# Conditioning steps in twos, filled waits between projection and MLP, last blocks computed half by half, in a float32 decoder step

## The chip, the cores and the metric

The kernel runs on one core of a Trainium2 chip. Its time is the device time of one execution in microseconds; the number to beat is the median of three executions. One of them is also recorded by the hardware profiler, and the times of single instructions below come from that recorded one.

## The reference

One inference step of a decoder layer in float32, width 2048, for 320 tokens at once: 256 of a prompt and 8 sequences of 8 new tokens. Two token mixers run side by side, HGRN2 (a recurrence with 8 heads of 128) and attention over a latent cache (MLA); their outputs are merged by sigmoid gates, projected, normalised and added to x. A squared-ReLU MLP of width 8192 follows, normalised and added in the same way. Shift, scale and gate of both halves come from a conditioning vector for each of the 9 sequences.

```python
mod = jax.nn.silu(c) @ w_ada[l] + b_ada[l]             # 2048 -> 12288, 9 rows
sh1, sc1, gt1, sh2, sc2, gt2 = split(mod, 6)
h = rms_norm(x, g_pre_mix) * (1 + sc1) + sh1
proj = h @ w_in                                        # HGRN2 and MLA inputs, gates
y_a = hgrn2(...) @ w_a_out
y_b = mla(...) @ w_b_out
merged = sigmoid(gate_a) * y_a + sigmoid(gate_b) * y_b
x = x + gt1 * rms_norm(merged @ w_o, g_post_mix)
h2 = rms_norm(x, g_pre_mlp) * (1 + sc2) + sh2
u = relu(h2 @ w_up)
x = x + gt2 * rms_norm((u * u) @ w_down, g_post_mlp)
```

## The kernel before

Everything large is a product of weights with activations that lie transposed on chip, 128 features by 320 tokens to a tile. `gemm` makes 256 output columns: for each 8 tiles of the inner dimension one load of 1 MB (`raw`, issued by SyncE, three buffers in `wraw`), split by ScalarE (`whi`, L151) and VectorE (`wlo`, L148) into a high and a low part in two pieces, each of four inner tiles, and then three matmuls for each tile and each of the two halves `m` of the columns (`mm3`). The two halves go in turn within an inner tile, so both are complete only with the last matmuls of a call.

The conditioning product `c @ w_ada` (`ada_gen`) is cut into 96 steps. In its later part a step is one load of 1 MB from the same three buffers and four matmuls of 32x512, which fill the four column groups of the array; the trace shows two rows for each of them, so a step is 8 rows named `aux<-raw,cT`. Every fourth step ends with a copy by ScalarE (`adarow`, L329), four transposes and a reduction on VectorE (L313). The steps are called from `tick`, after each 8 inner tiles of a `gemm` while `hook["every"]` is 1 (the HGRN stage: four head pairs `hp`, then two gate products), after each second while it is 2 (merge), and ten in a row between the output projection and the MLP, from a pool `fraw` of three buffers of their own. `tick` also advances the HGRN recurrence of the pair before by two pieces, so that its small matmuls (`X`, `qt,kt`, `rp`, `osq`) lie between those of the projections. The order of instructions on each engine is that in which a scheduler places them; `tc.issue_after(i)` holds an instruction behind `i`.

Between projection and MLP (the gap): `out_squares` squares the last output blocks and adds them to `ssum`, `out_tile` scales (`zg`) and transposes them, `out_store` copies them to `zt`, `tok_rstd` sums `ssum` over features by a matmul with ones and makes the reciprocal root `trr` (Ln on ScalarE at L220, Exp at L221, four small VectorE steps). The residual (`x`, L1337) is updated in six pieces, squared, turned into a second root `r`, scaled (L1348, back into `zt`), transposed and split to `gh`, `gl`, on which `w_up` starts. The last MLP chunk ends in the same chain, with `za` for the sum over chunks and `zu` for the output.

Of the kernel before, what the change touches and what calls it, by code (L numbers as in the profile page):

```python
# [1 line left out]

# [10 lines left out]
ALU = mybir.AluOpType  # L13
# [4 lines left out]
D = 2048  # L18
# [3 lines left out]
NS = NB * NT  # L22
N = NP + NS
P = 128
# [57 lines left out]
def tile_hgrn2_mla_step(  # L82
# [48 lines left out]
    def behind():  # L131

        return tc.issue_after(pe_last[0].ins)

    def mm(out, lhsT, rhs, start, stop):
# [8 lines left out]
    def add(out, a, b, eng=None):  # L144
        (eng or nc.vector).tensor_tensor(out=out, in0=a, in1=b, op=ALU.add)  # L145
# [52 lines left out]
    def gemm(w2d, kt0, nkt, c0, xh, xl, fine=False):  # L198

        ps = [bank(acc), bank(acc)]  # L200
        for r0 in range(0, nkt, 8):
            raw, rv = load_w(w2d, kt0 + r0, 8, c0, 256)
            for s in range(2):
                hv, lv = split_w(rv, 4 * s, 4, 256)
                for k in range(4):
                    kk = r0 + 4 * s + k
                    for m in range(2):
                        ms = slice(m * P, (m + 1) * P)
                        mm3(ps[m][:, 0:N], hv[:, k, ms], lv[:, k, ms], xh[:, kk], xl[:, kk],
                            kk == 0, kk == nkt - 1)  # L210
                if fine and s == 0:
                    advance(side["per"])
            tick()
        return ps
# [86 lines left out]
    araw = [sraw]  # L301

    turned = []

    def ada_turn():

# [10 lines left out]
    def ada_gen():  # L317

        for b0, nb in [(SC1, 2), (SH1, 2), (SC1 + 2, 2), (SH1 + 2, 2)] + \
                [(m + f, 4) for f in (4, 8, 12) for m in (SC1, SH1)] + [(b0, 4) for b0 in range(GT1, 96, 4)]:  # L320
            ps = bank()
            nk = 16 // nb
            for r0 in range(0, KF, nk):
                raw, rv = load_w(w_ada, r0, nk, b0 * P, nb * P, araw[0])
                for k in range(nk):
                    mm(ps[32 * (k % 4):32 * (k % 4 + 1), 0:nb * P], cT[:, r0 + k], rv[:, k], r0 + k < 4, r0 + k >= KF - 4)
# [901 lines left out]
    with pool("gt") as gt:  # L1228
        ah = gt.tile([P, NH, N], F32R, name="ah")
        al = gt.tile([P, NH, N], F32R, name="al")  # L1230
        bh = gt.tile([P, NH, N], F32R, name="bh")
        bl = gt.tile([P, NH, N], F32R, name="bl")
        for src, dh, dl in ((oB, bh, bl), (oA, ah, al)):
            for f0 in range(0, NH, 2):
                fs = slice(f0, f0 + 2)
                raw = dl[:, fs].bitcast(F32)
                nc.gpsimd.dma_start(out=raw, in_=src[:, fs])
                split(dh[:, fs], dl[:, fs], raw)
        hook["every"] = 2
        gates(4)  # L1240
        order = (2, 3, 4, 0, 1, 5, 6, 7)
        for n, g in enumerate(order):
            for w, vh, vl, nm in ((w_b_out, bh, bl, "gb"), (w_a_out, ah, al, "ga")):
                ps = gemm(w, 0, 8, 256 * g, vh, vl)
                s = gate[(nm, g)]
                for m in range(2):
                    mul(s[:, m], s[:, m], ps[m][:, 0:N])
            s, s2 = gate.pop(("gb", g)), gate.pop(("ga", g))
            add(s, s, s2, nc.gpsimd)
            split(mh[:, 2 * g:2 * g + 2], ml[:, 2 * g:2 * g + 2], s)  # L1250
            if n + 3 < 8:
                gates(order[n + 3])
# [20 lines left out]
    def out_tile(pl2, ps, f, m, m0, banks):  # L1273

        zg = pl2.tile([P, N], F32, name="zg")
        nc.scalar.activation(out=zg[:, 0:NP], in_=ps[:, 0:NP], func=AF.Copy, scale=mod[:, m0 + f, 0:1])
        mul(zg[:, NP:N].rearrange("p (b t) -> p b t", t=NT), ps[:, NP:N].rearrange("p (b t) -> p b t", t=NT),
            bc(mod[:, m0 + f, 1:9, None], [P, NB, NT]))
        for i, t0, n in TOK:
            dst = banks[0][:, m, i] if i < 2 else banks[1][0:NS, m]  # L1280
            transpose(dst, zg[:, t0:t0 + n], P)

    def out_banks():
        return bank().rearrange("p (m i c) -> p m i c", m=2, i=2), \
# [10 lines left out]
    def tok_rstd(pl, ssum):  # L1295
        ps = bank()
        for i, t0, n in TOK:
            mm(ps[0:n, i:i + 1], ssum[:, t0:t0 + n], ones[:, 0:1], True, True)
# [4 lines left out]
        mean_eps(xx[:, 0:2], ps[:, 0:2], D)  # L1303
        mean_eps(xx[0:NS, 2:3], ps[0:NS, 2:3], D)
        rstd_of(xx, tm, r)
        return r

    with pool("zp") as zp, pool("zp2", 2) as zp2, pool("fraw", 3) as fraw:
        zt = [zp.tile([P, D], F32, name=f"zt{i}") for i in range(3)]
# [2 lines left out]
        nc.sync.dma_start(out=x1[1], in_=x_prompt[0, P:NP])  # L1312
        nc.sync.dma_start(out=x1[2][0:NS], in_=xsm)
        for g in range(8):
            ps = gemm(w_o, 0, KF, 256 * g, mh, ml)
            bk = out_banks()
            for m in range(2):
                out_squares(zp2, ps[m][:, 0:N], 2 * g + m, ssum)
            for m in range(2):
                out_tile(zp2, ps[m][:, 0:N], 2 * g + m, m, GT1, bk)  # L1320
            lz = out_store(bk, zt, g)
            if g == 0:
                log_exp_tables(lz)
        r = tok_rstd(zp, ssum)
        araw[0] = fraw
        for _ in range(10):
            next(ada_steps)
        araw[0] = wraw
        ssq2 = zp.tile([P, 3, 2], F32, name="ssq2")
        xx2 = zp.tile([P, 3], F32, name="xx2")  # L1330
# [45 lines left out]
    with pool("ml1") as ml1, pool("ml2", 2) as ml2:  # L1376
# [4 lines left out]
        for c in range(NCH):  # L1381
            last = c == NCH - 1
            uh = ml2.tile([P, 8, N], F32R, name="uh")
            ul = ml2.tile([P, 8, N], F32R, name="ul")
            for g in range(4):
                ps = gemm(w_up, 0, KF, c * 1024 + 256 * g, gh, gl)
                for m in range(2):
                    u = ml2.tile([P, N], F32, name="u")
                    nc.scalar.activation(out=u, in_=ps[m][:, 0:N], func=AF.Relu)  # L1389
                    nc.scalar.activation(out=u, in_=u, func=AF.Square)  # L1390
                    split(uh[:, 2 * g + m], ul[:, 2 * g + m], u)
            if c == 5:
                hook["every"] = 0
                ada_turn()
                mod_gain(GT2, V_GPD, False)
            if last:
                gstack.close()
                tstack = ExitStack()
                tp = tstack.enter_context(pool("tp", 1, "right"))
                zt = [tp.tile([P, D], F32, name=f"zu{i}") for i in range(3)]  # L1400
            for g in range(8):
                ps = gemm(w_down, 8 * c, 8, 256 * g, uh, ul)
                bk = out_banks() if last else None
                for m in range(2):
                    f = 2 * g + m
                    if c == 0:
                        nc.scalar.copy(out=za[:, f], in_=ps[m][:, 0:N])
                    else:
                        add(za[:, f], za[:, f], ps[m][:, 0:N])
                    if last:  # L1410
                        out_squares(ml2, za[:, f], f, ssum)
                if last:
                    for m in range(2):
                        out_tile(ml2, za[:, 2 * g + m], 2 * g + m, m, GT2, bk)
                    out_store(bk, zt, g)
        r = tok_rstd(ml1, ssum)
        for q in range(4):
            fs = slice(q * 512, (q + 1) * 512)
            for i, t0, n in TOK:
# [37 lines left out]
```

## Time and profile before

| | us |
|---|---|
| median of three executions | 2150.62 (2146.13 to 2152.61) |
| profiled execution | 2150.7 |
| its span | 2148.8 |
| TensorE busy | 2097.8 (98%) |
| VectorE, ScalarE, GpSimd busy | 1075.0, 862.9, 167.6 |

The execution has 1.9 us around the span. The stages in the span: HGRN about 508 to 820, gates and merge to 1061, output projection to 1180, the gap to about 1231 where the first block of `w_up` ends, MLP to 2132, and a tail to the end. PE is the matmul stream of TensorE. A row of a timeline is a run of alike instructions: start, length of the run, engine, line, operation, output and inputs, count, and in brackets how long the engine stood idle before and what ended it. In the list of waits a row is who waited, for whom, the sum, the times and the longest. In the table of windows each row is a stretch with the busy time of each engine, the granted TensorE clock as a share of 2.4 GHz, and the load of the DMA engines.

### The profile page before, as it was taken

What the parts mean: (1) busy time and instruction counts of PE and PEld (TensorE: products, weight loads), DVE (VectorE), ACT (ScalarE), POOL (GpSimd) and SP (SyncE); (2) the same over time, 40 slices, a digit from 0 to 9 for tenths busy, and PEclk for the clock granted to TensorE, in tenths of its full rate; (3) what the DMA queues carried; (4) which work ended last, traced back from release to release, by engine and by line L of the source; (5) the groups of instructions that cost most, each with busy time, mean ns of one, the idle gap of its engine ahead of it and who ended that gap; (6) DMA issues with size and microseconds to landing.
All of it is one profiled execution on the core that took longest, in us unless ns stands there. A gap on an engine that the chain in (4) does not pass through costs nothing.

```text
span 2148.8 us, 34659 instructions
## 1 busy us (share of the span) xinstructions
PE 2097.8 (98%) x14605; PEld 1897.9 (88%) x14605; DVE 1075.0 (50%) x1673; ACT 862.9 (40%) x1312; POOL 167.6 (8%) x167
## 2 busy tenths in 40 slices
PE   6999999999999999999999899999999999999997
PEld 4788988557788889999999599999999999999996
DVE  3555854446665546533544633444444444444455
ACT  4332443334545434333344543424343433333343
POOL 0000101203332211000010000000000000000001
PEclk9999999999999999999999899999999999999998
DMA  9886554544776768766854555544544545445442
GB/s 291 310 291 228 175 192 140 214 132 138 240 233 209 244 215 273 240 196 221 274 162 144 189 177 178 155 145 149 157 141 154 153 143 155 147 148 157 144 151 70
DMA packets 327572, 401.69 MB, mean 187 GB/s; under 512 B 10984, under 2 KB 265528, under 8 KB 324600
## 3 DMA queue, kind: packets, MB, share of 16 engines
q1 hardware_dynamic: 301576, 362.82, 52.5%
q0 software_dynamic: 3584, 21.50, 2.9%
q10 hardware_dynamic: 22256, 15.16, 2.3%
q8 instruction: 115, 1.88, 0.4%
q14 instruction: 41, 0.34, 0.0%
HBM read 387.44 MB, written 12.01 MB: 186 GB/s over the span
## 4 chain that ended last, share of the span: by engine, by line
PE 87%; issue 4%; DVE 3%; DMA 3%; ACT 2%; POOL 1%; SPq 1%; DVEq 0%; ACTq 0%; POOLq 0%
PE acc L136 76%; PE aux L136 7%; PE aux L139 4%; DVE wlo L148 1%; ACT whi L151 1%; DMA raw<-in_w_in_dram 1%; DMA raw<-in_w_ada_dram 1%; POOL X L142 1%; DMA raw<-in_w_q_up_dram 1%; SPq L161 0%; DMA craw<-in_cache_ckv_dram,pidx 0%; DVE zu L1420 0%; DVE X L148 0%; DMA raw<-in_w_kv_up_dram 0%; DVE zg L142 0%
## 5 line engine op out<-in xcount | busy, mean ns | idle before, releaser
L148 DVE TENSOR_TENSOR wlo<-raw,whi 128x1024 fp32r<-128x1024 f32 (+1 forms) x493 | 604.0, 1230 | 704.2 <-ACT whi L151 703.6
L151 ACT CAST whi<-raw 128x1024 fp32r<-128x1024 f32 (+1 forms) x493 | 502.9, 1025 | 812.6 <-PE acc L136 681.7
L136 PE MATMUL acc<-hh,whi 128*128 128x320 f32 x1168 | 369.5, 317 | 2.5 <-DVE partb L145 1.2
L136 PE MATMUL acc<-hl,whi 128*128 128x320 f32 x1168 | 362.2, 310 | 0.0
L136 PE MATMUL acc<-hh,wlo 128*128 128x320 f32 x1168 | 361.9, 311 | 0.0
L136 PE MATMUL acc<-uh,whi 128*128 128x320 f32 x1024 | 316.7, 309 | 0.0
L136 PE MATMUL acc<-gh,whi 128*128 128x320 f32 x1024 | 316.7, 309 | 0.0
L136 PE MATMUL acc<-gh,wlo 128*128 128x320 f32 x1024 | 316.6, 309 | 0.0
L136 PE MATMUL acc<-gl,whi 128*128 128x320 f32 x1024 | 316.4, 309 | 0.0
L136 PE MATMUL acc<-uh,wlo 128*128 128x320 f32 x1024 | 316.1, 309 | 0.0
L136 PE MATMUL acc<-ul,whi 128*128 128x320 f32 x1024 | 316.1, 309 | 0.0
L136 PEld LDWEIGHTS acc<-hh,whi 128*128 128x128 f32 x1168 | 219.5, 188 | 33.7 <-issue 16.1
L136 PEld LDWEIGHTS acc<-hl,whi 128*128 128x128 f32 x1168 | 219.9, 188 | 2.4 <-DVE hl L148 0.8
L136 PEld LDWEIGHTS acc<-hh,wlo 128*128 128x128 f32 x1168 | 219.3, 188 | 3.0 <-DVE wlo L148 1.7
L136 PEld LDWEIGHTS acc<-gh,whi 128*128 128x128 f32 x1024 | 192.5, 188 | 1.9 <-ACT u L1390 0.8
L136 PEld LDWEIGHTS acc<-uh,whi 128*128 128x128 f32 x1024 | 192.6, 188 | 1.7 <-ACT u L1389 0.8
L136 PEld LDWEIGHTS acc<-gh,wlo 128*128 128x128 f32 x1024 | 192.6, 188 | 0.2
L136 PEld LDWEIGHTS acc<-gl,whi 128*128 128x128 f32 x1024 | 192.7, 188 | 0.0
L136 PEld LDWEIGHTS acc<-ul,whi 128*128 128x128 f32 x1024 | 192.4, 188 | 0.0
L136 PEld LDWEIGHTS acc<-uh,wlo 128*128 128x128 f32 x1024 | 192.4, 188 | 0.0
L136 PE MATMUL aux<-raw,cT 128*32 128x512 f32 (+1 forms) x832 | 117.0, 608 | 16.7 <-DVE tt L142 11.7
L145 POOL TENSOR_TENSOR ssum<-ssum,sqt 128x320 f32<-128x320 f32 x26 | 25.9, 997 | 981.3 <-ACT sqt L1270 980.3
(425 smaller groups left out, 2546.6 us busy)
## 6 DMA issues: line engine op xcount, KB each, us to landing
raw<-in_w_ada_dram SPq DMA_DIRECT2D x96, 1024.0 KB, 5.3
raw<-in_w_up_dram SPq DMA_DIRECT2D x64, 1024.0 KB, 5.7
raw<-in_w_down_dram SPq DMA_DIRECT2D x64, 1024.0 KB, 5.3
raw<-in_w_in_dram SPq DMA_DIRECT2D x60, 1024.0 KB, 5.3
raw<-in_w_o_dram SPq DMA_DIRECT2D x16, 1024.0 KB, 6.3
raw<-in_w_in_dram SPq DMA_DIRECT2D x20, 512.0 KB, 6.8
raw<-in_w_b_out_dram SPq DMA_DIRECT2D x8, 1024.0 KB
raw<-in_w_a_out_dram SPq DMA_DIRECT2D x8, 1024.0 KB, 5.3
```

What stands on the lines that cost most here:

```text
L136: pe_last[0] = nc.tensor.matmul(out, lhsT=lhsT, rhs=rhs, start=start, stop=stop)
L139: pe_last[0] = nc.tensor.transpose(out=out, in_=in_, identity=ident[:k, :k])
L142: (eng or nc.vector).tensor_tensor(out=out, in0=a, in1=b, op=ALU.mult)
L145: (eng or nc.vector).tensor_tensor(out=out, in0=a, in1=b, op=ALU.add)
L148: return (eng or nc.vector).tensor_tensor(out=out, in0=a, in1=b, op=ALU.subtract)
L151: nc.scalar.copy(out=hi, in_=src)
```

## The change

Three edits.

1. In the HGRN stage the conditioning steps are called two after every second tick, not one after every tick.
2. Between projection and MLP, two matmuls of 128x512 whose result nobody reads are put behind each of the steps 3 to 6 of the ten, and the copy `adarow` is held behind the Exp of the root. The steps of the gap are held behind the matmuls of the root (`pin`).
3. `gemm` gets `apart`: in the last 8 inner tiles of the last call, both pieces are split first, and then all matmuls of half 0 come before those of half 1. It is used for the last block of the projection and of the last MLP chunk. The last block's squares are no longer added to `ssum`; `tok_rstd` takes both tiles, and VectorE adds the second sum to the first. In the last chunk `out_tile` follows `out_squares` for each half.

```diff
-    hook = {"every": 0, "n": 0}
+    hook = {"every": 0, "n": 0, "do": 1}
...
-                next(ada_steps, None)
+                for _ in range(hook["do"]):
+                    next(ada_steps, None)
...
+            if apart and r0 == nkt - 8:
+                sp = [split_w(rv, 4 * s, 4, 256) for s in range(2)]
+                for m in range(2):
+                    ms = slice(m * P, (m + 1) * P)
+                    for k in range(8):
+                        hv, lv = sp[k // 4]
+                        mm3(ps[m][:, 0:N], hv[:, k % 4, ms], lv[:, k % 4, ms], xh[:, r0 + k], xl[:, r0 + k],
+                            r0 + k == 0, k == 7)
+                tick()
+                continue
...
-                    nc.scalar.copy(out=row[:, 0:nb * P], in_=ps[:, 0:nb * P])
+                    with behind_of(pinned[0]):
+                        nc.scalar.copy(out=row[:, 0:nb * P], in_=ps[:, 0:nb * P])
...
-    hook["every"] = 1
+    hook.update(every=2, do=2)
...
-        hook["every"] = 2
+        hook["do"] = 1
...
+            if f == KF - 1:
+                return t
...
+        for j, sq in enumerate(blocks):
+            for i, t0, n in TOK:
+                mm(ps[0:n, 3 * j + i:3 * j + i + 1], sq[:, t0:t0 + n], ones[:, 0:1], True, True)
+            for n, c0, c1 in ((P, 0, 2), (NS, 2, 3)):
+                if j == 0:
+                    mean_eps(xx[0:n, c0:c1], ps[0:n, c0:c1], D)
+                else:
+                    nc.vector.scalar_tensor_tensor(out=xx[0:n, c0:c1], in0=ps[0:n, 3 + c0:3 + c1], scalar=1.0 / D,
+                                                   in1=xx[0:n, c0:c1], op0=ALU.mult, op1=ALU.add)
...
-        for _ in range(10):
+        pinned[0], after_mm[0] = last_exp[0], pin
+        idle = bank(acc)
+        for n in range(10):
             next(ada_steps)
+            if 3 <= n < 7:
+
+                for _ in range(2):
+                    with behind():
+                        mm(idle, ident, cst[:, 0:512], True, True)
+                after_mm[0] = pe_last[0]
...
-                ps = gemm(w_down, 8 * c, 8, 256 * g, uh, ul)
+                ps = gemm(w_down, 8 * c, 8, 256 * g, uh, ul, apart=last and g == 7)
```

What SyncE issues at the end of the HGRN stage, before: weights of the projection (`in_w_in`) and of the conditioning (`in_w_ada`) alternate, one load each.

```order
L161 DMA raw<-in_w_ada_dram 128x4x512
L161 DMA raw<-in_w_in_dram 128x8x256
L161 DMA raw<-in_w_ada_dram 128x4x512
L161 DMA raw<-in_w_in_dram 128x8x256 x2
L161 DMA raw<-in_w_ada_dram 128x4x512
```

Now the loads come in twos, up to the last two of the stage.

```order
L165 DMA raw<-in_w_ada_dram 128x4x512 x2
L165 DMA raw<-in_w_in_dram 128x8x256 x2
L165 DMA raw<-in_w_ada_dram 128x4x512
L165 DMA raw<-in_w_in_dram 128x8x256 x2
L165 DMA raw<-in_w_ada_dram 128x4x512
```

The pairs take two of the three buffers one after the other.

TensorE in the first head pair of the recurrence, before. A count after x is of instructions; `X` and `qt,kt` are the recurrence, `acc` the projection.

```order
L136 MATMUL acc<-hh,wlo 128x320
L136 MATMUL aux<-raw,cT 32x512 x3
L136 MATMUL aux<-X 64x64 x10
L136 MATMUL aux<-qt,kt 64x64 x4
L136 MATMUL acc<-hh,whi 128x320
L136 MATMUL acc<-hl,whi 128x320
```

The same place now.

```order
L140 MATMUL acc<-hh,wlo 128x320
L140 MATMUL aux<-raw,cT 32x512 x7
L140 MATMUL aux<-X 64x64 x10
L140 MATMUL aux<-qt,kt 64x64 x4
L140 MATMUL acc<-hh,whi 128x320
L140 MATMUL acc<-hl,whi 128x320
```

The rest of a step stood before the recurrence's matmuls; now the rest of a step and a whole further one stand there.

TensorE in the gap, before, from the last matmul of the projection: `zg` transposes, `ssum` the sum for the root, `zt` the first transposes for the MLP.

```order
L136 MATMUL acc<-mh,wlo 128x320
L136 MATMUL aux<-raw,cT 32x512
L139 MATMUL aux<-ident,zg 128x128 x2
L139 MATMUL aux<-ident,zg 64x128
L139 MATMUL aux<-ident,zg 128x128 x2
L139 MATMUL aux<-ident,zg 64x128
L136 MATMUL aux<-cst,ssum 128x1 x2
L136 MATMUL aux<-cst,ssum 64x1
L136 MATMUL aux<-raw,cT 32x512 x7
L139 MATMUL aux<-ident,adarow 128x128 x4
L136 MATMUL aux<-raw,cT 32x512 x16
L139 MATMUL aux<-ident,adarow 128x128 x4
```

Now, from the last matmul of the projection to the end of steps 0 and 1, whose eight matmuls (1, 4 and 3) are in the piece.

```order
L140 MATMUL acc<-mh,wlo 128x320
L143 MATMUL aux<-ident,zg 128x128 x2
L143 MATMUL aux<-ident,zg 64x128
L140 MATMUL aux<-cst,ssum 128x1 x2
L140 MATMUL aux<-cst,ssum 64x1
L140 MATMUL aux<-cst,sqt 128x1 x2
L140 MATMUL aux<-cst,sqt 64x1
L140 MATMUL aux<-raw,cT 32x512
L143 MATMUL aux<-ident,zg 128x128 x2
L140 MATMUL aux<-raw,cT 32x512 x4
L143 MATMUL aux<-ident,zg 64x128
L140 MATMUL aux<-raw,cT 32x512 x3
```

And on from there, to the first transposes for the MLP.

```order
L143 MATMUL aux<-ident,adarow 128x128 x4
L140 MATMUL aux<-raw,cT 32x512 x8
L140 MATMUL acc<-cst,ident 128x512 x2
L140 MATMUL aux<-raw,cT 32x512 x4
L140 MATMUL acc<-cst,ident 128x512 x2
L140 MATMUL aux<-raw,cT 32x512 x4
L140 MATMUL acc<-cst,ident 128x512 x2
L143 MATMUL aux<-ident,adarow 128x128 x4
L140 MATMUL aux<-raw,cT 32x512 x4
L140 MATMUL acc<-cst,ident 128x512 x2
L143 MATMUL aux<-ident,zt_10108 128x128
```

The sum for the root stands ahead of step 0 now, with a second one (`sqt`) behind it. Steps 2 and 3 follow in one run (`x8`), two matmuls of 128x512 (`acc<-cst,ident`) stand behind each of the steps 3 to 6, and the transposes for the MLP follow the last two.

## Rows read from the trace of the kernel before

**Rows 1.** Waits of TensorE over the whole span.
```profile
PE aux L136 <- DMA raw<-in_w_ada_dram: 5.0, 4, 2.1
PE aux L139 <- DVE rp L1018: 3.1, 3, 1.8
PE aux L136 <- POOL X L142: 2.8, 2, 1.5
```

**Rows 2.** Timeline of TensorE around one conditioning step of the merge stage.
```profile
829.18 0.31 PE L136 MATMUL acc<-hl,whi 128*128 128x320 f32 x1
829.32 0.31 PE L136 MATMUL acc<-hh,wlo 128*128 128x320 f32 x1
829.56 1.07 PE L136 MATMUL aux<-raw,cT 128*32 128x512 f32 x8
830.56 0.41 PE L136 MATMUL acc<-hh,whi 128*128 128x320 f32 x1
```

**Rows 3.** Timeline of TensorE, a first piece of a step in the first head pair.
```profile
524.55 1.05 PE L136 MATMUL aux<-raw,cT 128*32 128x512 f32 x2
525.53 0.80 PE L136 MATMUL aux<-X 128*64 128x64 f32 x20
```

**Rows 4.** The tile `raw` on TensorE from 505 to 820: durations in ns, count.
```profile
L136 PE MATMUL aux<-raw,cT x224: 592/605/617, 514.7 to 814.8; 128*32 128x512 f32 x112
```

**Rows 5.** Timeline of TensorE in the gap.
```profile
1182.65 1.92 PE L136 MATMUL aux<-raw,cT 128*32 128x512 f32 x14
...
1189.04 1.06 PE L136 MATMUL aux<-raw,cT 128*32 128x512 f32 x8 [2.13 <-DMA raw<-in_w_ada_dram]
1191.74 1.71 PE L136 MATMUL aux<-raw,cT 128*32 128x512 f32 x8 [1.64 <-DMA raw<-in_w_ada_dram]
...
1200.02 5.04 PE L139 MATMUL aux<-ident,zt 128*128 128x128 f32 x16
```

**Rows 6.** Timelines of SyncE and ScalarE in the second head pair.
```profile
593.14 0.37 SPq L161 DMA_DIRECT2D raw<-in_w_in_dram  x1
598.57 2.00 ACT L151 CAST whi<-raw 128x1024 fp32r<-128x1024 f32 x2 [8.05 <-DMA raw<-in_w_in_dram]
```

**Rows 7.** All loads of `raw` from 505 to 820, from issue to landing.
```profile
DMA to landing us min/median/max: 5.1/5.3/5.6
```

**Rows 8.** Page, part 5: the low split on VectorE, count, busy time and mean.
```profile
L148 DVE TENSOR_TENSOR wlo<-raw,whi 128x1024 fp32r<-128x1024 f32 (+1 forms) x493 | 604.0, 1230 | 704.2 <-ACT whi L151 703.6
```

**Rows 9.** Timelines of ScalarE, VectorE and SyncE in the gap.
```profile
1184.62 0.59 ACT L329 COPY adarow<-aux 128x512 f32<-128x512 f32 x1 [1.10 <-PE aux L136]
...
1186.60 7.26 DVE L1337 SCALAR_TENSOR_TENSOR x<-zt,trr,x 128x1024 f32<-128x1024 f32 x6
...
1183.76 13.07 SPq L161 DMA_DIRECT2D raw<-in_w_ada_dram  x6
```

**Rows 10.** Windows of the gap.
```profile
1190.00:1192.00 2.00, 0.36 (x8) 0.16 (x8) 2.00 (x3) 1.91 (x5) 0.00 (x0) 1.00 1.04 386
1192.00:1194.00 2.00, 1.45 (x8) 0.00 (x0) 1.85 (x2) 1.92 (x5) 0.00 (x0) 0.51 1.05 389
1212.00:1214.00 2.00, 2.00 (x13) 0.61 (x13) 1.67 (x5) 1.64 (x3) 0.45 (x1) 0.87 0.00 0
```

**Rows 11.** Timeline of TensorE in the attention stage and behind the gap.
```profile
490.35 1.98 PE L136 MATMUL aux<-Ss,ckvs 64*128 64x512 f32 x4
...
1217.82 2.35 PE L139 MATMUL aux<-ident,zt 128*128 128x128 f32 x12
```

**Rows 12.** Timelines of VectorE and TensorE, an output block in the last MLP chunk.
```profile
2118.72 0.89 DVE L142 TENSOR_TENSOR zg<-za,mod 128x64 f32<-128x64 f32 x1
...
2118.73 1.24 PE L139 MATMUL aux<-ident,zg 128*128 128x128 f32 x6
```

**Rows 13.** Timeline of VectorE in the tail.
```profile
2134.14 0.49 DVE L145 TENSOR_TENSOR ssum<-ssum,sqt 128x320 f32<-128x320 f32 x1
...
2137.12 8.03 DVE L1420 SCALAR_TENSOR_TENSOR zu<-zu,trr,x 128x512 f32<-128x512 f32 x12
```

More of the change, by code (lines that the diff above doesn't have):

```diff
@@ L1 @@
-from contextlib import ExitStack
+from contextlib import ExitStack, nullcontext
 import concourse.bass as bass
@@ L133, in behind, with behind_of @@
         return tc.issue_after(pe_last[0].ins)
+    def behind_of(i):
+        return tc.issue_after(i.ins) if i is not None else nullcontext()
     def mm(out, lhsT, rhs, start, stop):
@@ L194, in tick, with gemm @@
             if hook["n"] % hook["every"] == 0:
-                next(ada_steps, None)
+                for _ in range(hook["do"]):
+                    next(ada_steps, None)
         advance(side["per"])
-    def gemm(w2d, kt0, nkt, c0, xh, xl, fine=False):
+    def gemm(w2d, kt0, nkt, c0, xh, xl, fine=False, apart=False):
         ps = [bank(acc), bank(acc)]
@@ L303, in tile_hgrn2_mla_step @@
     turned = []
+    pinned, after_mm = [None], [None]
     def ada_turn():
@@ L325, in ada_gen @@
                 for k in range(nk):
-                    mm(ps[32 * (k % 4):32 * (k % 4 + 1), 0:nb * P], cT[:, r0 + k], rv[:, k], r0 + k < 4, r0 + k >= KF - 4)
+                    with behind_of(after_mm[0]):
+                        mm(ps[32 * (k % 4):32 * (k % 4 + 1), 0:nb * P], cT[:, r0 + k], rv[:, k], r0 + k < 4, r0 + k >= KF - 4)
                 if r0 == KF - nk:
                     row = adap.tile([P, 512], F32, name="adarow")
-                    nc.scalar.copy(out=row[:, 0:nb * P], in_=ps[:, 0:nb * P])
+                    with behind_of(pinned[0]):
+                        nc.scalar.copy(out=row[:, 0:nb * P], in_=ps[:, 0:nb * P])
                     turned.append((b0, nb, row))
@@ L1280, in out_tile @@
             dst = banks[0][:, m, i] if i < 2 else banks[1][0:NS, m]
-            transpose(dst, zg[:, t0:t0 + n], P)
+            with behind_of(pin):
+                transpose(dst, zg[:, t0:t0 + n], P)
     def out_banks():
@@ L1293, in out_store, with tok_rstd @@
         return last_
-    def tok_rstd(pl, ssum):
+    def tok_rstd(pl, blocks):
         ps = bank()
-        for i, t0, n in TOK:
-            mm(ps[0:n, i:i + 1], ssum[:, t0:t0 + n], ones[:, 0:1], True, True)
         xx = pl.tile([P, 3], F32, name="trx")
@@ L1302, in tok_rstd @@
         nc.vector.memset(xx, 1.0)
[L1303 to L1304 removed]
+        for j, sq in enumerate(blocks):
[7 more added lines that the diff above has]
+                                                   in1=xx[0:n, c0:c1], op0=ALU.mult, op1=ALU.add)
+        behind_r = pe_last[0]
         rstd_of(xx, tm, r)
[L1306 removed]
+        return r, behind_r
     with pool("zp") as zp, pool("zp2", 2) as zp2, pool("fraw", 3) as fraw:
@@ L1314, in tile_hgrn2_mla_step @@
         for g in range(8):
-            ps = gemm(w_o, 0, KF, 256 * g, mh, ml)
+            ps = gemm(w_o, 0, KF, 256 * g, mh, ml, apart=g == 7)
             bk = out_banks()
+            pin = None
             for m in range(2):
-                out_squares(zp2, ps[m][:, 0:N], 2 * g + m, ssum)
-            for m in range(2):
-                out_tile(zp2, ps[m][:, 0:N], 2 * g + m, m, GT1, bk)
+                lsq = out_squares(zp2, ps[m][:, 0:N], 2 * g + m, ssum)
+                if 2 * g + m == KF - 1:
+                    r, pin = tok_rstd(zp, (ssum, lsq))
+                out_tile(zp2, ps[m][:, 0:N], 2 * g + m, m, GT1, bk, pin)
             lz = out_store(bk, zt, g)
@@ L1401, in tile_hgrn2_mla_step @@
             for g in range(8):
-                ps = gemm(w_down, 8 * c, 8, 256 * g, uh, ul)
-                bk = out_banks() if last else None
+                ps = gemm(w_down, 8 * c, 8, 256 * g, uh, ul, apart=last and g == 7)
+                bk, pin = out_banks() if last else None, None
                 for m in range(2):
@@ L1410, in tile_hgrn2_mla_step @@
                     if last:
-                        out_squares(ml2, za[:, f], f, ssum)
+                        lsq = out_squares(ml2, za[:, f], f, ssum)
+                        if f == KF - 1:
+                            r, pin = tok_rstd(ml1, (ssum, lsq))
+                        out_tile(ml2, za[:, f], f, m, GT2, bk, pin)
                 if last:
-                    for m in range(2):
-                        out_tile(ml2, za[:, 2 * g + m], 2 * g + m, m, GT2, bk)
                     out_store(bk, zt, g)
-        r = tok_rstd(ml1, ssum)
         for q in range(4):
```

4 lines of the change are left out of this document (2 added, 2 removed).

## The prediction

> **What bounds the kernel now.** I read the list of waits first, then the timelines of the three places that the change touches, then the windows of the gap for the clock. The list of waits says that TensorE is nearly always at work: its largest waits in the stretch of the change are some 5.0 us for conditioning weights in the gap, and 3.1 and 2.8 us for VectorE (`rp`) and GpSimd (`X`) in the HGRN stage [rows 1]. The reader is to see there that no other engine bounds the kernel as a whole, so that an edit is worth what it takes out of TensorE's own stream, and only in a few places what it takes out of a wait. Everything is added to the profiled execution, 2150.7 us, of which 2148.8 is the span and 1.9 lies around it; it agrees with the median of 2150.62 within 0.1. I hold a change of less than 0.3% (6.45 us) for one that a measurement of this kernel can't tell from none, as the three executions lie 6.5 apart.
>
> **Steps in twos.** The timeline around one step shows what it costs TensorE to stand alone between projection matmuls. The two matmuls before it start 0.14 apart (829.18, 829.32), the next one behind it starts at 830.56, 1.24 after the last: a step alone takes 1.24 - 0.14 = 1.10 us [rows 2]. Directly behind another step it takes less: 14 rows, that is three matmuls of one step and all four of the next, took 1.92 [rows 5], and the piece of a step alone takes about 1.05 however short (two rows took 1.05, and the next work began 0.98 after them [rows 3]). So the second step adds 1.92 - 1.05 = 0.87. The stage has 224 rows, 28 steps [rows 4], and four of them are cut in two by recurrence matmuls, each as in [rows 3]: 32 stands of 1.10 are 35.2 us. In the new order there are 13 pairs of 1.10 + 0.87 = 1.97, one more cut after its first matmul (1.97 + 1.05), and no other cut: 28.6. The stream gets 6.6 us shorter.
>
> Not all of it reaches the end. In three of the four head pairs and in the gate products TensorE doesn't wait, and 26 of the 32 stands lie there: 26 x 1.10 = 28.6 before, 12 x 1.97 = 23.6 after, 5.0 us that I count in full. In the first head pair (1.6 us) TensorE waits for the recurrence, most of `X` 2.8 and `rp` 3.1 lies there [rows 1]; earlier arrival is there mostly a longer wait, and where a step that stood between two pieces of the recurrence is gone, its 1.10 no longer covers the wait for GpSimd. I take nothing of the 1.6, and 5.0 for the edit. The bounds are 2.0 (the waits for `X` grow by 1.6 each time and the saving of that pair is gone) and 7.5 (all 6.6, and the waits shrink by 0.9 as recurrence work moves ahead of a step).
>
> What the pairs do to the loads: each pair takes two of three buffers, so that the second of the next two projection loads is issued when the first step of a pair is done, not a whole `gemm` block ahead. From that issue it has the second step (0.87), one block of 48 matmuls (48 x 0.14 = 6.7 us, with the distance of two in [rows 2]) and the recurrence's matmuls between (some 1.4, an estimate from the row of 0.80 in [rows 3] and its like), 9.0 in all. It needs 5.4 to the cast (593.14 to 598.57 [rows 6]), 1.0 for the cast (2.00 for two) and 1.23 for the low part [rows 8]: 7.7. Landing was 5.1 to 5.6 through the whole stage [rows 7]. So 1.3 us are left and I take no wait; the price if they are not there is a rival below. ScalarE waited 8.05 for that load before [rows 6], which costs nothing as long as TensorE has split weights in hand.
>
> **The gap.** Before, TensorE comes to the refilled conditioning loads too early: the first is issued at 1183.76, when step 0 ends [rows 9], and lands at 1189.04, the next 2.70 later [rows 5]. TensorE is busy 0.36 of the 2 us from 1190 on, and from 1192 the granted clock is 0.51, that is 1.2 in place of 2.4 GHz; it is back in the window from 1212, whose mean of 0.87 says that 0.26 of the 2 us were at half [rows 10]. The price shows in the rows: 16 transposes 5.04 (0.315 each) [rows 5], 12 at full clock 2.35 (0.196) [rows 11].
>
> The new order step by step. The root: its sum is taken ahead of step 0 and the `adarow` copy, which waited 1.10 for TensorE at 1184.62 and stood in front of the Exp [rows 9], is behind it now. I get the first piece of `x` at 1185.5 in place of 1186.60. But step 0 ends about 1.25 later, at 1185.0, since both sums and two transposes stand ahead of it; and the refill starts when step 0 ends, so step 3 can start at 1185.0 + 5.3 = 1190.3. The earlier root is hidden by that. Then four times a step and two matmuls of N = 512: two such took 1.98 [rows 11] (four rows, two matmuls), so four times about 3.0, and 0.5 for the `adarow` transposes: the transposes for the MLP start at 1190.3 + 12.0 + 0.5 = 1202.8, in place of 1200.02. That is 2.8 lost for filling, more than loads 2.70 apart ask for. If the clock holds, what took 1200.02 to 1212.26 at half, 12.24 us, takes 6.12 of TensorE's time: 6.12 - 2.8 = 3.3 won at most. The transposes also wait for scaling, eviction and split on VectorE and ScalarE, which no clock makes faster, so I take 1.5. Bounds: 3.3 won, and 3 lost where the fillers run at half and the clock comes back no earlier.
>
> Here a rule is to be weighed. The windows show the fall of the clock after a stretch in which TensorE did two short steps in 5 us and waited for loads, and the rise behind the first dense projection matmuls of `w_up`, well after the transposes had begun at 1200.02. The Trainium skill, "TensorE: Matmul & The Clock Gate", section "HAM oscillation — how this bites in real kernels", says that waits for DMA between short bursts of matmuls throttle the clock, each time anew. This trace agrees for the first half (0.51 from 1192). By that rule filling from step 3 on may be too late, as the wait before step 3 is still empty (by the durations above from 1185.0 + 0.9 + 0.5 + 1.1 = 1187.5, after steps 1 and 2 and the transposes between, to 1190.3); that is the first rival.
>
> **Last blocks by halves.** In the last block of the projection and in each of the eight output blocks of the last MLP chunk half 0 can be scaled and transposed earlier, but half 1 sets the end: its `zg` on VectorE took 0.89 (beside GpSimd's sum) and the transposes 1.24 [rows 12]; I count nothing, -0.5 to +0.7. In the tail one 0.49 sum of squares (2134.14) leaves the chain to the final pass at 2137.12 [rows 13], and a VectorE step of about 0.2 on three columns joins it, with up to three copies of 0.3 ahead: 0.4 won, 0 to 1.
>
> **Sum.** 5.0 + 1.5 + 0.0 + 0.4 = 6.9 us less: 2150.7 - 6.9 = 2143.8.
>
> **Rivals.**
> *The clock falls all the same.* For it: the empty 2.8 us before step 3, and 8-row steps alone in front of it. Against: the fillers start 1.0 us behind that. The first pair then runs at half (1.98 more) and a step too (0.87 more): the gap is 2.8 worse than forecast, 1.3 slower than before; 2150.7 - 5.0 + 1.3 - 0.4 = 2146.6. That is no change by the bound.
> *Everything is saved.* The first head pair's waits go with the steps (7.5 in place of 5.0) and the gap gives 2.3: 2150.7 - 7.5 - 2.3 - 0.4 = 2140.5. For it: the steps moved there stood ahead of recurrence matmuls. Against: the waits are for GpSimd and VectorE, not for TensorE.
> *The ring starves.* If a projection load that now shares the engines with two conditioning loads takes one load's time more (2.70, the distance in [rows 5]), its 1.3 us of room turn into a wait of 1.4 for each of the 13 pairs: 18.2, and 2143.8 + 18.2 = 2162.0, slower than before. It decides from 6.9 / 13 = 0.53 a pair. Against: the landings of [rows 7] spread by 0.5 only, while loads of both kinds were in flight together.
>
> **How the numbers follow.** Forecast 0.50, own range 2141 to 2147; clock falls 0.25; everything saved 0.12; ring starves 0.13. The range of 8 in 10 goes from 2139.5, below everything saved, to 2153, which leaves out most of the starving ring. Faster by over 0.3% means under 2144.2: a bit over half of the forecast (0.28), all of the second rival (0.12) and a little of the first (0.03), 0.43. Slower by over 0.3% means above 2157.1: most of the ring, 0.10. The rest, 0.47, is no change, with the forecast at its edge.
>
> **What would show it.** In the timeline of the changed kernel: rows of 16 for a pair of about 1.93, not 2.1; no wait of TensorE for `whi` or `wlo` between 520 and 815 (one of 0.5 or more a pair would make the ring right); the gate stage ending some 5 us earlier; the first wait before the MLP ending at about 1190 less those 5, the clock at 1.00 from there to the first `w_up` matmul (0.5 in a window makes the first rival right), 16 transposes in about 3.1; the final pass 0.4 earlier against the last matmul. The forecast is wrong if the merge stage starts less than 2 us earlier, or if the distance from the last projection matmul to the first finished block of `w_up` grows.

## The result, and the profile after

The changed kernel takes 2155.86 us in the median of 8 executions, the kernel before 2149.71 beside it: ratio 1.003, 95% interval 1.0021 to 1.004. It is slower by about what I called the bound of no change, not faster by as much; the forecast of 2143.8 and the range up to 2153 are both missed. A second set on another chip gave 2158.18 against 2149.75, ratio 1.0043 (1.003 to 1.0057).

To see where the time went I cut each profiled execution at rows that all kernels have: the first `olat` matmul ahead of the HGRN stage, the last `osq` of that stage, the first matmul with `bh` (merge), the last of `w_o`, the first `u` of `w_up`, the last 384 matmuls (the last chunk's `w_down`), the last matmul. Each entry is the difference of two starts.

| us | before | after | difference | after, second profile |
|---|---|---|---|---|
| to the first `olat` | 498.00 | 500.14 | +2.14 | 500.95 |
| to the last `osq` | 309.33 | 303.79 | -5.54 | 302.93 |
| to the merge | 38.50 | 48.66 | +10.16 | 48.32 |
| to the last of `w_o` | 334.23 | 334.21 | -0.02 | 334.19 |
| gap, to the first `u` | 51.49 | 50.82 | -0.67 | 48.70 |
| to the last chunk's `w_down` | 836.59 | 836.59 | 0.00 | 836.59 |
| last chunk's `w_down` | 64.25 | 65.74 | +1.49 | 65.80 |
| tail | 16.4 | 15.7 | -0.7 | 15.7 |

The first row is code that the change doesn't touch; over all the profiles here it lies between 495.74 and 504.16. It is not plain scatter, though: the six profiles with a pair at the end of the HGRN stage and its conditioning loads have the six largest values (499.30 to 504.16), the other twelve 495.74 to 499.08. TensorE's matmuls in that row are the same in these six and in the kernel before, so this is seen and not explained, and 2 to 3 us of the slowdown stay outside the account below. Rows two and three belong together, since the last pair stands behind the last `osq` where single steps stood ahead of it: +4.6 us (+3.4 in the second profile), where I forecast -5.0.

The waits of TensorE over the span, in the kernel after, beside [rows 1]:

```profile
PE aux L143 <- DVE rp L1036: 6.1, 3, 3.2
PE aux L140 <- DMA raw<-in_w_ada_dram: 5.0, 3, 2.3
PE acc L140 <- ACT whi L155: 4.8, 1, 4.8
PE aux L143 <- DVE zg L146: 3.0, 5, 0.6
PE aux L140 <- POOL X L146: 2.2, 2, 1.3
```

Two lines are new, `whi` with one wait of 4.8 and `zg` with five of 0.6, and `rp` has doubled. The `whi` wait is the seam between the HGRN stage and the merge. TensorE there, after:

```profile
812.57 1.92 PE L140 MATMUL aux<-raw,cT 128*32 128x512 f32 x16
828.70 1.06 PE L140 MATMUL aux<-raw,cT 128*32 128x512 f32 x8
834.53 0.64 PE L140 MATMUL acc<-hh,whi 128*128 128x320 f32 x1 [4.77 <-ACT whi L155]
```

A pair costs 1.92, as forecast. What came late is read from SyncE's loads (a row of two shows the first issue and the stretch to the end of the second), then ScalarE's cast, after:

```profile
802.38 11.68 SPq L165 DMA_DIRECT2D raw<-in_w_in_dram  x2
814.55 0.37 SPq L165 DMA_DIRECT2D raw<-in_w_ada_dram  x1
816.14 6.71 SPq L165 DMA_DIRECT2D raw<-in_w_in_dram  x2
```

```profile
819.01 2.00 ACT L155 CAST whi<-raw 128x1024 fp32r<-128x1024 f32 x2 [4.16 <-DMA raw<-in_w_in_dram]
833.43 1.04 ACT L155 CAST whi<-raw 128x1024 fp32r<-128x1024 f32 x1 [4.24 <-DMA raw<-in_w_in_dram]
```

The same loads before, with the cast of the last of them, and the windows of the kernel before just ahead of them:

```profile
802.87 3.10 SPq L161 DMA_DIRECT2D raw<-in_w_in_dram  x2
814.85 0.37 SPq L161 DMA_DIRECT2D raw<-in_w_ada_dram  x1
815.42 8.32 SPq L161 DMA_DIRECT2D raw<-in_w_in_dram  x2
```

```profile
835.17 1.05 ACT L151 CAST whi<-raw 128x1024 fp32r<-128x1024 f32 x1 [2.29 <-DMA raw<-in_w_in_dram]
```

```profile
804.00:808.00 4.00, 4.00 (x25) 2.56 (x24) 2.49 (x10) 0.00 (x0) 0.00 (x0) 1.00 0.94 298
808.00:812.00 4.00, 4.00 (x29) 4.00 (x28) 0.97 (x3) 1.06 (x2) 0.00 (x0) 1.00 0.69 226
```

Before, the second of the two loads goes out at 805.6, 3.10 - 0.37 behind the first. After, its buffer is held for the pair, and it goes out at 813.7, when the pair's first step is done. So three loads of 1 MB start between 813.7 and 816.2, after a stretch in which the DMA engines have little to do, and from 817.49 on GpSimd loads the outputs of both mixers (2.6 MB). I call these GpSimd loads the burst. It also comes nearer: before, it starts 5.14 behind the load of 815.42; after, 1.35 behind that of 816.14. GpSimd issues it right behind a product that needs the last `osq`, and this `osq` now stands ahead of the pair. GpSimd's first four loads, before and after:

```profile
820.56 2.24 POOL L1237 DMA_DIRECT2D bl<-oB  x4
```

```profile
817.49 2.24 POOL L1255 DMA_DIRECT2D bl<-oB  x4
```

The windows of the kernel after:

```profile
808.00:812.00 4.00, 4.00 (x29) 4.00 (x28) 3.03 (x4) 3.74 (x5) 0.00 (x0) 1.00 0.21 61
812.00:816.00 4.00, 4.00 (x33) 2.39 (x32) 3.52 (x7) 2.86 (x5) 1.03 (x1) 1.00 0.24 54
820.00:824.00 4.00, 4.00 (x29) 4.00 (x28) 2.36 (x2) 1.23 (x3) 1.33 (x3) 1.00 1.06 403
828.00:832.00 4.00, 1.76 (x14) 0.66 (x12) 1.65 (x2) 1.03 (x2) 0.00 (x0) 1.00 1.04 368
832.00:836.00 4.00, 1.11 (x3) 0.71 (x4) 1.49 (x2) 2.57 (x4) 0.00 (x0) 0.63 1.08 363
836.00:840.00 4.00, 4.00 (x16) 4.00 (x17) 4.00 (x6) 3.52 (x6) 0.00 (x0) 0.52 0.41 116
```

The last two columns are to be read: 54 to 61 GB/s up to 816, then 363 to 403. The load issued at 816.14 is cast at 833.43, 17.3 us later. The column before the last two, the clock, falls to 0.52 behind the wait.

### The profile page after: what moved, and what is told of

Same layout as the page of the kernel before. It is cut to its first block, busy times and chain, and to the rows that moved or that the text cites. A ratio compares the mean times of both kernels' runs of the same rounds, so it can differ in the third digit from the quotient of the medians.

```text
span 2155.7 us, 34715 instructions
## 1 busy us (share of the span) xinstructions
PE 2097.7 (97%) x14633; PEld 1907.4 (88%) x14633; DVE 1068.1 (50%) x1675; ACT 863.3 (40%) x1312; POOL 167.5 (8%) x167
## 4 chain that ended last, share of the span: by engine, by line
PE 84%; DMA 5%; issue 4%; DVE 4%; ACT 1%; SPq 1%; POOL 0%; DVEq 0%; ACTq 0%; POOLq 0%
PE acc L140 74%; PE aux L140 7%; PE aux L143 3%; DMA raw<-in_w_in_dram 3%; DVE wlo L152 1%; DMA raw<-in_w_ada_dram 1%; ACT whi L155 1%; DVE X L152 0%; SPq L165 0%; DVE zu L1458 0%; DMA raw<-in_w_q_up_dram 0%; POOL X L146 0%; DMA raw<-in_w_kv_up_dram 0%; DVE zg L146 0%; DVE Sn L1181 0%
## 5 line engine op out<-in xcount | busy, mean ns | idle before, releaser
L152 DVE TENSOR_TENSOR wlo<-raw,whi 128x1024 fp32r<-128x1024 f32 (+1 forms) x493 | 597.5, 1217 | 727.5 <-ACT whi L155 726.8
L140 PE MATMUL aux<-raw,cT 128*32 128x512 f32 (+1 forms) x832 | 107.6, 587 | 16.5 <-DVE tt L146 11.5
```

The source lines that it names most:

```text
L152: return (eng or nc.vector).tensor_tensor(out=out, in0=a, in1=b, op=ALU.subtract)
```

## The experiments

Theory A: the last pair alone does it, by holding back one load ahead of that burst. B: every pair starves the ring (the three buffers of `raw`). C: the pairs are sound and the loss is in gap and last blocks.

**Pairs alone**, and everything but the pairs:

```diff
 before + steps in twos:          hook.update(every=2, do=2)
 after with single steps:    -    hook.update(every=2, do=2)
                             +    hook.update(every=1, do=1)
```

> The kernel before with the conditioning steps in twos and nothing else. Theory A (the last pair holds two buffers just before the merge, one projection load is issued late and lands among the loads of the attention and HGRN outputs, 7.6 us lost there; the pairs before it win 3.0): 4.6 us slower than before, a wait of TensorE for whi of about 4.8 us near 830 and the clock at 1.2 GHz behind it, no such wait elsewhere between 520 and 815. Theory B (every pair starves the ring a little): slower by 5 or more with waits for whi or wlo at several pairs. Theory C (the pairs are sound and the loss is in the gap and the last blocks): 3 to 5 us faster than before.

> The changed kernel with the steps one by one again in the HGRN stage. Theory A and B: the gap gives -0.7, the last MLP chunk +1.5 and the tail -0.7, so 0.1 from before, 2 us either way, no wait for whi near 830. Theory C: as slow as the changed kernel, 4 to 6 us slower than before.

Pairs alone: 2151.86 against 2149.76, ratio 1.0006 (0.9994 to 1.0018); the profiled execution has a wait for `whi` of 4.7 and 48.64 to the merge. Without pairs: 1.0004 (0.9994 to 1.0014), 38.49 to the merge and no such wait. That is A's place, and C falls; A's price for the pairs alone (4.6) is not met in the median. The pairs alone are profiled twice more below.

**Single steps in the last gate product only**, then also the old order in the blocks of the last chunk:

```diff
         gates(2)
+        hook.update(every=1, do=1)
         gates(3)
...
-                        out_tile(ml2, za[:, f], f, m, GT2, bk, pin)
+                        if g == 7:
+                            out_tile(ml2, za[:, f], f, m, GT2, bk, pin)
                 if last:
+                    if g < 7:
+                        for m in range(2):
+                            out_tile(ml2, za[:, 2 * g + m], 2 * g + m, m, GT2, bk)
```

> The changed kernel with pairs until the second gate product, and single steps in the last one (four steps before the merge). Theory A: the wait near 830 is gone, the wins of the pairs before it stay, about 2.5: 2.4 us faster than before (-2.5 - 0.7 + 1.5 - 0.7) and 8 to 9 faster than the changed kernel. Theory B: it gets back a sixth of the loss, still 4 or more slower than before. Theory C: no change against the changed kernel.

> As e3_single_end, and the first seven output blocks of the last MLP chunk square both halves before they scale and transpose them, as before the change. If the order of squares and tiles by halves costs 0.36 us a block there (VectorE's zg late, 0.6 of wait in each of five blocks), this is 1.5 to 2.5 us faster than e3_single_end and 4 to 5 faster than before. If the waits in these blocks only replace other work, no difference from e3_single_end.

The first gives 1.0002 (0.9992 to 1.0012): with two of 14 pairs undone the 0.3% are gone, 38.49 to the merge, no wait for `whi`. B falls as a wait of TensorE. But the pairs that are left win only 1.4 from the stage's start to the merge, not 2.5. The second gives 0.9989 (0.9978 to 0.9999): the last chunk is back at 64.24, 1.5 less, and the waits for `zg` there are gone.

**What the burst needs.** The loads of both mixers' outputs left out:

```diff
-                nc.gpsimd.dma_start(out=raw, in_=src[:, fs])
+                nc.gpsimd.memset(raw, 0.0)
```

> The changed kernel with the loads of both mixers' outputs (bl, al, 2.6 MB through GpSimd's queue) left out: these tiles are set to zero, so the attention and HGRN parts of the output are missing. The pair at the end of the HGRN stage stays. If the wait near 830 needs both, the late issue of the projection load and the head loads beside it: the wait for whi goes to under 0.5 us and the time falls by 6 to 9 us against the changed kernel. If the occupied buffers alone make it: the wait stays at 4 us or more.

0.999 (0.9979 to 1.0), that is 0.95 us under the kernel before, where the changed kernel was 6.2 and 8.4 over it: the time comes back with the last pair in place. There is no wait for `whi`, and 42.20 to the merge in place of 48.66. The windows of this kernel, which show the DMA engines done by 824 and idle:

```profile
820.00:824.00 4.00, 4.00 (x29) 3.92 (x27) 4.00 (x7) 4.00 (x7) 1.07 (x2) 1.00 1.00 345
824.00:828.00 4.00, 4.00 (x22) 2.01 (x21) 4.00 (x6) 2.94 (x4) 0.00 (x0) 1.00 0.01 2
```

So the wait takes both, the last pair and the 2.6 MB beside it: 48.66 - 42.20 = 6.5 us. Of this 4.77 + 0.36 are waited. The half clock behind costs some 2.2 more, an estimate: from 834.5 to 839.7 the matmuls start 0.27 apart, not 0.147. The kernel without the loads gives about 1 back elsewhere, since its next step is cut in two. The last pair does two things, it holds one load back and it lets the burst start nearer (1.35 behind the load that is then late; 3.43 with single steps at the end). No run holds the one fixed and moves the other, so their shares are open.

**Is it paid by every execution?** The changed kernel and the pairs alone again, then pairs alone against the same with single steps in the last gate product:

> The changed kernel once more, another execution in the profile. If the wait before the merge is part of every execution: whi waited for by 4 us or more near 830, 48 us or more from the last osq of the HGRN stage to the merge (38.5 before), and again 5 to 7 us slower than before. If it was that one execution's: under 2 us of wait.

> The kernel before with the pairs alone, another execution in the profile. Its twelve times lay in two groups, about 2148 and 2155. If the wait before the merge comes in only some executions of it: now either no wait for whi near 830 and a time near 2148, or the wait and a time near 2155. If the wait is in all, the two groups come from the gap before the MLP: the wait is there at either time, and the gap is 47 to 48 or 51 to 54 us long.

> The kernel before with pairs in the HGRN stage up to the second gate product and single steps in the last one; gap and last blocks as before. Against e1_third on the same chip. If the wait before the merge is paid by every execution: 5 to 7 us faster than e1_third, 1 to 1.5 faster than before. If it is paid only by the slow group of e1's executions: medians within 3 us of each other, and the lowest times equal.

> The kernel before with the pairs alone, the partner of e11_pairs_then_singles. Paid by every execution: no time of it under e11's median. Paid by some: a third to a half of its times as low as those of e11.

All five profiles of kernels with a pair at the end and all their loads show the wait (4.7 to 5.1) and 48.3 to 49.7 to the merge; none of the others has it. On one chip the pairs alone take 2153.68 and those with single steps at the end 2148.53, 5.2 us apart; two of their 12 times lie under the other's median. So it is paid always or nearly so. What makes the two groups of times is not settled. The gap of the old code took 51.49, 47.60, 51.82, 47.26 and 52.31 in the five profiles that have it, a spread of the right size; but the execution of 2156.43, one of the upper group, has the short gap of 47.60. Open, too, is why the medians of the pairs alone lie only 1.9 to 3.8 above the kernel before, while their three profiles are 5.1 to 8.4 longer from the first `olat` to the merge.

**What becomes of the pairs' own gain.** All pairs on the other tick, just ahead of `rp` (with the blocks of the last chunk in the order of before); and pairs and single steps whose loads are left out in the HGRN stage (`araw[0]` is `None` there), so that their matmuls read a tile that is already on chip:

```diff
+    hook.update(every=2, do=2, n=hook["n"] + 1)
...
-                raw, rv = load_w(w_ada, r0, nk, b0 * P, nb * P, araw[0])
+                if araw[0] is None:
+                    rv = hh[:, 0:8, 0:256].bitcast(F32).rearrange("p (k j) c -> p k j c", j=2)
+                else:
+                    raw, rv = load_w(w_ada, r0, nk, b0 * P, nb * P, araw[0])
```

> As e4_tiles_last, but all 14 pairs are kept and called on the other of the two ticks, so that a pair stands just ahead of the transposes of rp in each head pair, and the last pair one block of 48 matmuls further from the merge. If the pairs lost their gain because steps had covered TensorE's wait for rp on VectorE: waits for rp sum to under 3 us (e3_single_end 6.9), the HGRN stage is 2 to 4 us shorter than before the change (e3_single_end 1.4), 1 to 2.5 us faster than e4_tiles_last. If the last pair starves the merge wherever it stands: a wait for whi near 830 and 5 us slower than e4_tiles_last.

> The changed kernel with the loads of the 28 conditioning steps of the HGRN stage left out: their matmuls read a resident tile, so the modulation that they compute is wrong. All three buffers are for the projection's loads. To be read against e10_singles_no_loads, which has the same loads out and the steps one by one. If the pairs' gain was eaten by the ring (a projection load issued only when a pair is done, its cast and low part late on VectorE, the copy of rp behind them): the waits for rp go back to 3 us or less, no wait for whi, and this is 4.5 to 6.5 us faster than e10_singles_no_loads. If VectorE's own work sets rp: waits for rp stay at 6 us or more, and the difference is 1 to 3 us.

> The changed kernel with single steps in the HGRN stage and the loads of these 28 steps left out (the modulation that they compute is wrong). The reference for e9_pairs_no_loads. As single steps didn't wait for their loads before: from the start of the HGRN stage to the merge within 1 us of e2_no_pairs; if the loads slow the stage by taking bandwidth from the projection's, 2 us or more less.

On the other tick no `whi` wait comes, but `rp` is still waited for by 6.9 in all and the stage with the way to the merge is 1.2 shorter: the time's ratio to before is 0.9994 (0.9983 to 1.0005), and covering `rp` with a pair was a wrong idea. Without their loads, pairs take 2144.89 and single steps 2151.58, 6.7 us apart, 4.5 of it between `olat` and the merge. That looks like the forecast's 5.0, but it does not show that the loads eat the gain: 2.4 of the 4.5 is that the single steps without loads are slower to the merge than with them (350.23 against 347.83; the order of the stage's matmuls came out differently), and the pairs without loads need 345.73, no less than some of the pairs with them (344.69 to 347.83 in the six profiles with pairs up to the second gate product). `rp` is waited for by 7.2 and 8.1 in these two, with the loads by 6.1 in the changed kernel and 3.2 in the one without pairs. So what lengthens the wait for `rp` is not settled. One path can be read in the kernel after, second head pair, ScalarE and VectorE:

```profile
606.49 1.05 ACT L155 CAST whi<-raw 128x1024 fp32r<-128x1024 f32 x1 [2.21 <-DMA raw<-in_w_in_dram]
607.44 0.73 ACT L985 ACTIVATE fg<-fg 128x640 f32<-128x640 f32 x1
```

```profile
607.57 1.23 DVE L152 TENSOR_TENSOR wlo<-raw,whi 128x1024 fp32r<-128x1024 f32 x1 [2.35 <-ACT whi L155]
608.72 1.53 DVE L988 TENSOR_TENSOR_SCAN bb<-cst,fg 128x320 f32<-128x320 f32 x2
611.28 2.10 DVE L152 TENSOR_TENSOR X<-bb 128x256 f32<-128x256 f32 x6
613.29 0.42 DVE L1036 COPY rp<-kt 128x192 f32<-128x192 f32 x2
```

ScalarE waits for the load that goes out when a pair is done, and the recurrence's `fg`, the scan and `rp` stand behind that cast in the two engines' order. TensorE then waits for `rp`, in the second and third head pair, before and after:

```profile
614.58 0.64 PE L139 MATMUL aux<-ident,rp 128*96 128x128 f32 x4 [0.75 <-DVE rp L1018]
698.81 0.64 PE L139 MATMUL aux<-ident,rp 128*96 128x128 f32 x4 [0.55 <-DVE rp L1018]
```

```profile
613.61 0.64 PE L143 MATMUL aux<-ident,rp 128*96 128x128 f32 x4 [3.16 <-DVE rp L1036]
698.26 0.64 PE L143 MATMUL aux<-ident,rp 128*96 128x128 f32 x4 [1.83 <-DVE rp L1036]
```

**The gap.** One idle matmul for each step, none, and the first again, also with single steps in the whole stage (all with the blocks of the last chunk in the order of before):

```diff
-                for _ in range(2):
+                for _ in range(1):
...
-            if 3 <= n < 7:
+            if n < 0:
```

> As e4_tiles_last, with one idle matmul of 128x512 behind each of the steps 3 to 6, not two. Each takes 0.95, a step 1.0, and loads land 2.7 apart, so one fits into the wait and two overrun it. If the fillers cost more than they save: the transposes for the MLP start about 2.5 earlier in the gap, the gap from the last projection matmul to the first finished w_up half is 47 to 48.5 us (e3_single_end 49.2 with the clock held), 1 to 2 us faster than e4_tiles_last. If one filler doesn't hold the clock: half rate up to w_up and a gap of 50 to 52.

> As e4_tiles_last, without the idle matmuls. If the fillers are worth what the changed kernel has them for: the clock is at 1.2 GHz for most of the gap, the gap is 51 to 52 us, 1 to 2 slower than e4_tiles_last. If the slow clock of the gap costs about as much as the fillers take (the kernel before was seen with 51.5, the same gap code in e1_pairs_only with 47.6): no difference from e4_tiles_last within its interval.

> Single steps through the whole HGRN stage, one idle matmul in the gap, first seven output blocks of the last MLP chunk in the order of before; the rest as the changed kernel. If pairs that don't reach the merge are worth the 1.4 us that e3_single_end showed: about 1 us slower than e5_again, and 2 to 3 faster than before (gap -1 to -3, tail -0.7). If the gap's gain is chance: level with before but for the tail.

> The version with pairs up to the second gate product, one idle matmul behind each of four steps, and the blocks of the last MLP chunk in the order of before, a second time: 2 to 4 us faster than before if the gains of its parts (HGRN 0 to 1.5, gap 1 to 3, tail 0.7) hold.

Windows of the gap, with one idle matmul (second run, one of four short falls of the clock told of below) and with none:

```profile
1183.00:1193.00 10.00, 7.67 (x37) 1.32 (x36) 7.92 (x16) 6.71 (x14) 0.00 (x0) 0.83 1.04 388
1193.00:1203.00 10.00, 8.94 (x52) 4.37 (x48) 7.84 (x31) 4.76 (x8) 0.82 (x2) 1.00 0.89 322
```

```profile
1187.00:1197.00 10.00, 6.92 (x28) 1.31 (x28) 8.10 (x23) 5.71 (x13) 0.00 (x0) 0.52 1.04 378
1197.00:1207.00 10.00, 9.58 (x36) 3.51 (x36) 6.20 (x21) 4.42 (x8) 0.85 (x2) 0.50 0.65 231
```

With none the clock stays at half and the gap takes 53.57 (one profile). With one it takes 48.51, 48.52 and 48.52; with two, 48.70 to 50.82 in nine profiles, 49.6 in the mean; the old code's mean of five is 50.1.

The granted clock, read in windows of 2 us, sorts these. Without idle matmuls it falls in all six profiles: to 0.50 for about 10 us in the two short gaps of the old code, for 20 to 24 us in its other three and in the one with none. With them it stays at 1.00 in eight of twelve and is at half for 3 to 4 us in the other four. So the idle matmuls hold the clock or bring it back early, and the second one gives back 1.1 of the 1.6 us that one wins over the old code. The times alone don't show this: with one idle matmul 2147.22, with none 2147.97, on the same chip.

The ratios to the kernel before: one idle matmul 0.999 (0.9976 to 1.0005) and again 0.9983 (0.9973 to 0.9994); with single steps 0.9996 (0.9985 to 1.0007); none 0.9993 (0.998 to 1.0005). The version with pairs up to the second gate product, one idle matmul, the old order in the last chunk and halves in the very last blocks is faster than the kernel before by 0.17% in its second run, 2145.23 against 2149.91; the interval of its first run includes no change. That pairs add to it is likely (2145.23 against 2149.10 on the same chip, with overlapping intervals) but small: over six profiles they take 0 to 3.1 off, 1.3 in the mean.

## Why the prediction was wrong, step by step

*Steps in twos: the step that failed.* The duration (14 rows or 16 in 1.92) was right, and 13 whole pairs with one more cut after its first matmul came out as foreseen. (Of the four cut steps before, two are cut by projection matmuls, not by the recurrence, which leaves the sum as it is.) What failed is "1.3 us are left and I take no wait". I worked out the room of a steady pair, with the landing of 5.1 to 5.6 [rows 7], and asked the trace for loads up to 820. The stage's ring does not end there. In the kernel before, the load issued at 823.4 is cast at 835.17, 11.8 us later, and costs nothing only because it was needed at 837.6; the burst was there to be seen. My rival of the starving ring had the mechanism and the side, with the wrong place: 1.4 at each of 13 pairs, where the runs showed 6.5 once, at the last one. The term of -5.0 measured +4.6 in one profile and +3.4 in the other.

*"I count in full".* This failed as well. I put most of the wait for `rp` into the first head pair and none into the others; of its three waits [rows 1] two, 0.75 and 0.55, lie in the second and third. They grew to 3.16 and 1.83, by 3.7 in all, and `rp` over the stage from 3.1 to 6.1. The pairs that don't reach the merge are worth 1.3 in the mean, not 5.0. The growth of these two waits is as large as the difference, but the waits of the first head pair shrank at the same time (`X` from 2.8 to 2.2, its `rp` from 1.79 to 1.07), so it is not the whole. The way from `olat` to the merge less all waits of TensorE over 0.2 us is 340.6 before and 336.0 to 337.7 in those six profiles, 3 to 4.5 us less where the count gave about 6; where the rest of the saving goes stays open.

*The gap.* The root came 1.1 earlier against the last matmul, as forecast (`x` at 1192.20, 5.40 after it; before 1186.60, 6.54 after it). The refill came later and the clock fell once more in the empty wait before step 3, after:

```profile
1197.45 1.19 PE L140 MATMUL aux<-raw,cT 128*32 128x512 f32 x8 [2.29 <-DMA raw<-in_w_ada_dram]
1198.56 2.08 PE L140 MATMUL acc<-cst,ident 128*128 128x512 f32 x2
...
1211.08 0.95 PE L143 MATMUL aux<-ident,zt 128*128 128x128 f32 x5
```

```profile
1198.00:1200.00 2.00, 2.00 (x10) 0.84 (x3) 2.00 (x3) 1.89 (x5) 0.00 (x0) 0.56 1.04 392
1204.00:1208.00 4.00, 4.00 (x18) 1.40 (x17) 3.81 (x15) 0.59 (x1) 0.00 (x0) 1.00 1.04 328
```

It was back by 1204, behind the first idle matmuls. The rule that the prediction cites from the Trainium skill ("TensorE: Matmul & The Clock Gate", "HAM oscillation — how this bites in real kernels") agrees with this profile and with the kernel without fillers. But six of the nine profiles of this gap code, one of the changed kernel's two among them, held 1.00 through that wait, so here the fall does not come each time. The term was -1.5 and measured -0.7 with the fall and -2.8 without it, so its size hung on the execution. The 2.8 for overrunning fillers, which I saw and let stand, is real in part: with one idle matmul the gap is 1.1 shorter in the mean.

*Last blocks.* "I count nothing, -0.5 to +0.7" was mis-sized: +1.5, and the old order of the blocks takes it back (64.24). In the chunk after, TensorE:

```profile
2091.12 0.55 PE L143 MATMUL aux<-ident,zg 128*128 128x128 f32 x3
2092.41 0.30 PE L143 MATMUL aux<-ident,zg 128*64 128x128 f32 x1 [0.60 <-DVE zg L146]
2092.70 0.38 PE L143 MATMUL aux<-ident,zg 128*128 128x128 f32 x2
```

Before, six transposes ran as one [rows 12]; now the 64-column one of half 1, whose `zg` VectorE finishes at 2092.36 behind a low part, stands ahead of the two others. The tail gave 0.7 for 0.4: the final pass, after, beside [rows 13]:

```profile
2143.96 8.03 DVE L1458 SCALAR_TENSOR_TENSOR zu<-zu,trr,x 128x512 f32<-128x512 f32 x12
```

It starts 4.01 after the last matmul of 2139.95; before it was 4.73 after 2132.39.

## What to carry to other kernels

When loads of two streams share a ring of buffers, grouping the one stream's work delays the other's next load (here from 805.6 to 813.7); price it at the place where the room is smallest, which here was the seam where another transfer begins, and ask the trace for landings past the end of the stage. A matmul saved in a stream whose engine waits now and then for another engine can be worth less than its duration, even where those waits are small: here 1.3 us of 5.0. A filler should fit into the wait that it fills: one that overran gave back 1.1 of 1.6 us.

## What was not expected of the hardware

A load of 1 MB landed in 5.1 to 5.6 us through the HGRN stage [rows 7], and its cast began 17.3 us after its issue when 2.6 MB of GpSimd's loads and up to three further loads of 1 MB were in flight beside it, at 363 to 403 GB/s in all. The same gap with the same code took 47.26 to 52.31 in five executions, depending on how long the granted clock stayed at 0.50, and with two idle matmuls the clock fell in three executions and held in six, so that one profile doesn't price it.
